# One fused decoder block on one core: a broadcast load moved behind a weight load, the work around the values' products reordered, two products swapped, upper values at other steps

## The chip, the core and the metric

The kernel runs on one core of a Trainium2 chip. A core has five engines with an instruction queue each: TensorE (PE, matmuls), VectorE (DVE), ScalarE (ACT), GpSimd (POOL) and SyncE (SP), which here only issues transfers. An engine works through its queue in order, and waits on semaphores for the others. The metric is the device time of one execution in microseconds; lower is better.

## The reference

One block of a decoder on 1024 tokens of 1024 features, in float32. The input is normalised (RMSNorm) and projected to queries, keys and values of 8 heads, to `u` and `vg` of a gated MLP, and to 8 forget logits. Forgetting attention, chunked spatial gating, and then a gated MLP with a causal convolution follow:

```python
xn = rmsnorm(h, norm_mix_g[layer])
proj = xn @ w_in[layer]                       # q, k, v, u, vg, forget logits
log_f = jax.nn.log_sigmoid(proj[..., G_END:] + b_forget[layer])
att = forgetting_attention(q, k, v, log_f)    # softmax(q k^T / 8 + c_i - c_k, causal) v, c = cumsum(log_f)
u, vg = split(jax.nn.gelu(proj[..., V_END:G_END]))
...
# gating: vg is normalised per group of 64 features, then per chunk of 128 tokens
w = w_s * jnp.tril(jnp.ones((CHUNK, CHUNK)))
mixed = jnp.einsum('gij,bnjgd->bnigd', w, vc) + b_s.T[None, None, :, :, None]
sg = u * mixed
h = h + jnp.concatenate([att, sg], axis=-1) @ w_out[layer]
h = h + conv_ffn(rmsnorm(h, norm_ffn_g[layer]), ...)   # (silu(g) * a) @ w_down, width-3 causal conv before
return rmsnorm(h, norm_final_g)
```

The change touches the part from the end of the `u`, `vg` and value projections to the first attention heads; the MLP behind it stays as it is.

## The kernel before

**Products.** Each float32 operand is split into a high part and a low part in the matmul's own type: ScalarE copies the high part (`act.copy`, line 157), VectorE subtracts it to get the low part (line 163). A product is then three matmuls: high by high, high by low, low by high. Many products are built as in Strassen's scheme: sums and differences of quarter matrices are multiplied, and the results added. The names T1 to T4, B11 to B22 stand for such quarters of the activations, and S1 to S4, A11 to A22 for those of a weight. `tmul` (line 267) multiplies one chunk of 128 rows, `product` (line 515) one quarter of the query and key weights, `vmul` (line 845) one of the values.

**Values, first half.** `wva` (two loads) and `wvk` hold weights for the values and the forget logits (264 columns, of which the last 8 are the logits). `vsum` adds two parts of them; `high` and `low` split them. T3-half and B22-half (matmuls of 264 columns, line 267) multiply them into the banks `S` and `S2`. Around them stand the gates: `gelu` on ScalarE, squares on ScalarE and group sums (`reduce`) on VectorE, a square root and a reciprocal of `gms`, and `norm`, which multiplies `vg` by it. `copies` stores the partial values and the logits (`vx`, `zf`). `rb` is 1/rms of every token, broadcast to all partitions: ScalarE stores it to `rbd` in HBM, SyncE loads it back (line 411). `emit` multiplies the keys and queries by it.

**Queries and keys.** `Weights(i)` loads a quarter of the query and key weights (two loads of 512 KB), `sums` and `last_sum` add quarters on GpSimd (lines 537 to 547), `split` splits them. `q1`, `q2` and four `qk_step` compute queries and keys of four pairs of heads, by products into the banks qa to qd. `forget` makes the log-sigmoid of the logits (table loads, Exp, Ln on ScalarE), `forget_sums` its running sums (matmuls at lines 601 and 602).

**Values, second half, and gating.** Weights `wvl` give the three products S2 x T2, A22 x T4 and S1 x T1 (line 845). Their results, with the partial values from `vx`, become values of the lower tokens (stored as `vd`, read back) and of the upper four heads (stored to `vu`). `evac_v` scales a tile of values into V: high part on ScalarE (line 733), low part on VectorE (line 737). `spatial` (line 792) multiplies eight groups of `vg` by the masked spatial weights `ws`, and gates `u` with the result: the first half on VectorE (`A<-pb`), the second half on ScalarE (into a temporary `pt`) and GpSimd (line 802). `turn_sg` transposes it (line 815), and the first head's logits follow (lines 967 and 968).

**Heads.** Each head has five steps with logits, softmax parts (`CUSTOM_DVE` at line 980, Exp at line 990), transposes (line 1015) whose results are split (lines 1016 and 1017) and products with V (line 1031). In steps 5 to 12 one tile of the upper four heads' values goes through `evac_v`.

**What sets the order.** While `act.on` and `dve.on` are true, each ScalarE or VectorE instruction is tied behind the one that the program wrote before it, so the order in the text is the order on the engine. With them false, the scheduler orders by its own costs, and `after(tc, later, earlier)` adds a single edge. `behind(inst, key)` ties to a gate stored under a key. SyncE issues loads and stores in the order of the text, as their buffers come free: `raw` has four buffers, `whl` four, `wy` two, `pt` three; a new tile of a name waits for the last reader of the buffer that it takes. Banks of `bank` and `sbank` are four each.

Of the kernel before, what the change touches and what calls it, by code (L numbers as in the profile page):

```python
# [14 lines left out]
P = 128  # L15
# [7 lines left out]
FCFG = ("b", 4, 4)  # L23

# [42 lines left out]
def block_kernel(ctx: ExitStack, tc: tile.TileContext, xT, xtok, wuv, wv0, wva, wvk, wvl, wqk, cpk, bfv,  # L67
# [341 lines left out]
    rb = sb("t01", [P, 1024])  # L409
    act.dma_start(out=rbd.rearrange("a p -> p a"), in_=rstd1)  # L410
    sp.dma_start(out=rb, in_=rbd.rearrange("a b -> (a b)").unsqueeze(0).to_broadcast((P, 1024)))
# [58 lines left out]
    w3 = [high(own_[0][:, k, :], 264) for k in range(2)]  # L470
    reduce(sq[0], 1, 0)
# [3 lines left out]
    for k in range(2):  # L475
        low(w3[k], own_[0][:, k, :])
    reduce(sq[1], 1, 2)
    w3 += [high(own_[0][:, k, :], 264) for k in (2, 3)]
    sq = [square(0, 0), square(0, 2)]
    dve.tensor_tensor(out=va[1][:, 0:1056], in0=va[0][:, 0:1056], in1=va[1][:, 0:1056], op=ALU.add)  # L480
    vsum(1)
    for k in (2, 3):
        low(w3[k], own_[0][:, k, :])
    reduce(sq[0], 0, 0)
    w4 = [high(own_[1][:, 0, :], 264)]
    reduce(sq[1], 0, 2)
    low(w4[0], own_[1][:, 0, :])
    act.activation(gms, gms, AF.Sqrt, bias=eps[:, 0:1], scale=1.0 / 64)
    dve.reciprocal(gms, gms)
# [3 lines left out]
    w4.append(high(own_[1][:, 1, :], 264))  # L493
    low(w4[1], own_[1][:, 1, :])
    for m in range(4):
        dve.tensor_tensor(out=ut[1][:, m, :], in0=B[m], in1=ut[1][:, m, :], op=ALU.subtract)
    for k in (2, 3):
        w4.append(high(own_[1][:, k, :], 264))
        behind_ = low(w4[k], own_[1][:, k, :])
    for m in range(4):  # L500
        gelu(ut[1][:, m, :], 4 + m)
    for hf in (1, 0):
        for t in (0, 2):
            norm(hf, t)
# [3 lines left out]
    copies(S, vx[1], 1)  # L508
# [10 lines left out]
    class Weights:  # L519


        def __init__(self, i):
            self.a, self.b = sb("raw", [P, 2, 512]), sb("raw", [P, 2, 512])
            sp.dma_start(out=self.a, in_=wqk[i, :, 2:4, :])
            sp.dma_start(out=self.b, in_=wqk[i, :, 0:2, :])
# [25 lines left out]
    W[0].split("A11", "A12")  # L551
    W[0].sums(behind_)
# [4 lines left out]
    act.on = dve.on = False  # L557
# [8 lines left out]

    qa = q1(0, "c")
    q2 = psq("a")
    product(q2, W[0].w["A12"], "B21", True)
# [13 lines left out]
    def forget_sums(c, r):  # L583
# [7 lines left out]
        act.activation(e, e, AF.Exp, scale=-1.0)  # L591
        x = act.activation(e, e, AF.Ln, bias=one[:, 0:1])
# [25 lines left out]
    fg = forget()  # L618
    tq, tk = sb("G", [P, 2, 1024]), sb("G", [P, 2, 1024])

    def emit(t, dst, i, parts, src=None):
        for o in parts:
            if dst is kd:
                dve.tensor_tensor(out=t[:, 1, o], in0=t[:, 1, o], in1=rb[:, o], op=ALU.mult)
            x = t[:, 1, o] if src is None else src
            act.copy(t[:, 0, o].bitcast(F32R), x)
            dve.tensor_tensor(out=t[:, 1, o], in0=x, in1=t[:, 0, o], op=ALU.subtract)
            for j in range(2):
                sp.dma_start(out=dst[2 * i + j].rearrange("s d t -> d s t")[:, :, o], in_=t[j * 64:(j + 1) * 64, :, o])
# [16 lines left out]
    def qk_step(i, qa, nxt):  # L646
# [5 lines left out]
        dve.tensor_tensor(out=u2, in0=qb, in1=x1, op=ALU.subtract)  # L652
        qc = psq("c")
        product(qc, w.w["S3"], "T3", True)
        dve.tensor_tensor(out=tk[:, 1, hi], in0=u2, in1=qc, op=ALU.add)
        w.split("S1")
        if i > 0:
            product(qa, w.w["A12"], "B21", False)
            emit(tq, qd, i, (lo,), qa)
        else:  # L660
# [6 lines left out]
        if i == 3:  # L667
            gates["keys"] = d
# [15 lines left out]
        if i == 3:  # L684
            gates["queries"] = d
# [6 lines left out]
    def gate_gain(hf):  # L692
# [3 lines left out]
        for t in (0, 2):  # L696
            v = vgt[hf][:, t:t + 2, :]
            behind(dve.tensor_tensor(out=v, in0=v, in1=gg[0].unsqueeze(1).to_broadcast((P, 2, 512)), op=ALU.mult), "queries")

    W[0].split("S2", "S3")  # L700
    fsum = forget_sums(*fg)
    next(fsum)
    for i in range(4):
# [6 lines left out]
    behind(dve.tensor_tensor(out=l21, in0=l21, in1=l22, op=ALU.add), "keys")  # L710
    behind(dve.tensor_tensor(out=l11, in0=l11, in1=l21, op=ALU.add), "keys")

    def pairs(t, gate=None):
        return [tsplit(t[:, 512 * j:512 * j + 512], gate, tag="whl") for j in range(2)]

    vw = {"S2": pairs(l11, "keys"), "A22": pairs(l22, "queries")}
    gate_gain(0)
# [3 lines left out]
    for i in range(2):  # L721
# [1067 lines left out]
```

## Time and profile before

| | |
|---|---|
| median of three executions | 1066.36 us (1063.12 to 1066.54) |
| profiled execution, its own time | 1066.44 us |
| its span in the profile | 1064.7 us |
| TensorE busy | 1043.8 us (98%) |
| VectorE busy | 892.9 us (84%) |
| ScalarE busy | 564.2 us (53%) |
| GpSimd busy | 223.5 us (21%) |
| mean granted TensorE clock | 0.996 |

The profile shows one execution. A row of a timeline gives the start in us from the span's start, the duration, the engine, the line, the operation with its output and inputs, and how many like it follow in a row; in brackets stands the idle time of the engine before it and the instruction that ended the wait. Names are those of the program's buffers, not of its variables: the banks of TensorE are `pb`, `ps`, `qa` to `qd`, `pl`; `G` holds among others the weights `wva` and the gates `vg`, `A` the gates `u`, `x` the value sums, `raw` loaded weights, `whl` and `wy` split ones. Lines 45 and 52 are the helper that ties instructions, so many operations have that line. A row of the table of stretches gives its bounds, then for each engine its busy time and, in brackets, its instructions, and at the end the granted clock, the busy share of the transfers and GB/s.

### The profile page before, as it was taken

What the parts mean: (1) busy time and instruction counts of PE and PEld (TensorE: products, weight loads), DVE (VectorE), ACT (ScalarE), POOL (GpSimd) and SP (SyncE); (2) the same over time, 40 slices, a digit from 0 to 9 for tenths busy, and PEclk for the clock granted to TensorE, in tenths of its full rate; (3) what the DMA queues carried; (4) which work ended last, traced back from release to release, by engine and by line L of the source; (5) the groups of instructions that cost most, each with busy time, mean ns of one, the idle gap of its engine ahead of it and who ended that gap; (6) DMA issues with size and microseconds to landing.
All of it is one profiled execution on the core that took longest, in us unless ns stands there. A gap on an engine that the chain in (4) does not pass through costs nothing.

```text
span 1064.7 us, 14262 instructions
## 1 busy us (share of the span) xinstructions
PE 1043.8 (98%) x4997; PEld 873.1 (82%) x4997; DVE 892.9 (84%) x1298; ACT 564.2 (53%) x1003; POOL 223.5 (21%) x169
## 2 busy tenths in 40 slices
PE   9999999989999999999999999999999999999997
PEld 6988888878888888888888888888888888888886
DVE  6897786878878869998999989989998775998774
ACT  6776532356866746654444444444444454444654
POOL 0000331230410740054333333323322000000000
PEclk9999999999999999999999999999999999999999
DMA  9624358768456345132344423322321899433342
GB/s 325 234 10 170 106 164 237 219 200 233 142 164 176 128 150 201 65 99 99 99 140 161 155 88 110 109 93 95 123 106 62 286 333 308 128 94 96 139 127 100
DMA packets 68491, 161.66 MB, mean 152 GB/s; under 512 B 9142, under 2 KB 10278, under 8 KB 68420
## 3 DMA queue, kind: packets, MB, share of 16 engines
q1 hardware_dynamic: 67108, 160.71, 47.5%
q8 instruction: 39, 0.64, 0.3%
q14 instruction: 32, 0.26, 0.1%
q10 hardware_dynamic: 1312, 0.04, 0.1%
HBM read 115.68 MB, written 45.05 MB: 151 GB/s over the span
## 4 chain that ended last, share of the span: by engine, by line
PE 83%; DVE 8%; ACT 4%; DMA 2%; issue 2%; SPq 0%; POOL 0%; ACTq 0%; DVEq 0%
PE k L1602 20%; PE qc L1342 11%; PE qa L1342 11%; PE qd L1342 11%; PE qb L1342 5%; PE pb L1031 2%; PE pb L1015 2%; PE ps L267 2%; PE pl L967 1%; PE pl L968 1%; PE pf L1055 1%; PE qc L515 1%; PE pf L1056 1%; PE pf L1057 1%; PE qd L515 1%
## 5 line engine op out<-in xcount | busy, mean ns | idle before, releaser
L1602 PE MATMUL k<-whb,wha 128*128 128x512 f32 (+1 forms) x936 | 209.9, 386 | 0.0
L1602 PEld LDWEIGHTS k<-whb,wha 128*128 128x128 f32 x936 | 174.1, 188 | 35.8 <-DVE wha L163 0.2
L1342 PE MATMUL qc<-xT,whb 128*128 128x512 f32 x540 | 129.9, 389 | 0.2 <-ACT whb L157 0.2
L1342 PE MATMUL qa<-xB,wha 128*128 128x512 f32 x528 | 127.4, 390 | 0.0
L1342 PEld LDWEIGHTS qc<-xT,whb 128*128 128x128 f32 x540 | 101.3, 188 | 21.6 <-ACT whb L157 0.5
L1342 PEld LDWEIGHTS qa<-xB,wha 128*128 128x128 f32 x528 | 98.8, 188 | 20.8 <-DVE wha L163 0.4
L157 ACT CAST wha<-sg 128x512 fp32r<-128x512 f32 x77 | 47.8, 622 | 96.6 <-PE k L1602 86.1
L157 ACT CAST whb<-sg 128x512 fp32r<-128x512 f32 x82 | 50.5, 618 | 87.6 <-PE qc L1342 67.3
L163 DVE TENSOR_TENSOR wha<-sg,wha 128x512 fp32r<-128x512 f32 x77 | 52.8, 688 | 38.8 <-ACT wha L157 38.7
L1342 PE MATMUL qd<-xB,whb 128*128 128x512 f32 x264 | 63.7, 389 | 0.0
L1342 PE MATMUL qd<-xT,whb 128*128 128x512 f32 x264 | 63.7, 389 | 0.0
L1016 ACT CAST pt<-pb 128x512 fp32r<-128x512 f32 x72 | 40.4, 585 | 41.1 <-PE pb L1015 34.6
L1342 PE MATMUL qb<-xT,whb 128*128 128x512 f32 x252 | 61.0, 389 | 0.0
L163 DVE TENSOR_TENSOR whb<-sg,whb 128x512 fp32r<-128x512 f32 x82 | 57.0, 697 | 4.4 <-ACT whb L157 4.3
L1226 POOL TENSOR_TENSOR sg<-raw 128x512 f32<-128x512 f32 x20 | 30.7, 1533 | 140.3 <-DVE whb L163 80.2
L1342 PEld LDWEIGHTS qd<-xT,whb 128*128 128x128 f32 x264 | 49.5, 188 | 10.5 <-DVE u L1449 0.3
L1342 PEld LDWEIGHTS qd<-xB,whb 128*128 128x128 f32 x264 | 49.5, 188 | 10.3
L1017 DVE TENSOR_TENSOR pt<-pb,pt 128x512 fp32r<-128x512 f32 x72 | 47.4, 687 | 11.0 <-ACT pt L1016 10.9
L1342 PEld LDWEIGHTS qb<-xT,whb 128*128 128x128 f32 x252 | 47.2, 188 | 10.1 <-DVE whb L163 0.3
L1031 PE MATMUL pb<-pt,V 128*128 128x512 f32 (+3 forms) x192 | 50.1, 365 | 0.4 <-DVE pt L1017 0.3
L1229 POOL TENSOR_TENSOR sg<-sg,raw 128x512 f32<-128x512 f32 x20 | 33.3, 1666 | 63.4 <-DVE whb L163 63.4
L1227 POOL TENSOR_TENSOR sg<-sg,raw 128x512 f32<-128x512 f32 x20 | 35.1, 1757 | 47.2 <-issue 44.6
(406 smaller groups left out, 2256.3 us busy)
## 6 DMA issues: line engine op xcount, KB each, us to landing
raw<-wup SPq DMA_DIRECT2D x44, 512.0 KB
sg<-hx SPq DMA_DIRECT2D x77, 256.0 KB
hx<-hs SPq DMA_DIRECT2D x44, 256.0 KB
hx<-ca SPq DMA_DIRECT2D x35, 256.0 KB
xT<-wdn SPq DMA_DIRECT2D x28, 256.0 KB
x<-kd SPq DMA_DIRECT2D x24, 256.0 KB
A<-xtok SPq DMA_DIRECT2D x8, 512.0 KB
raw<-wqk SPq DMA_DIRECT2D x8, 512.0 KB
```

The source lines that it names most:

```text
L157: act.copy(h, src)
L163: return eng.tensor_tensor(out=l, in0=src, in1=f32(h), op=ALU.subtract)
L267: pe.matmul(banks[m], xs(n, xi, k)[:, ms], w[:, wi, :], start=(first and k == 0 and c == 0 and (own or m % 2 == 0)), stop=(k == 3 and c == ...
L515: pe.matmul(ps, w[:, wi, ks], xs(n, xi, k), start=(first and c == 0), stop=(c == 11), skip_group_check=True)
L1016: casts.append(act.copy(pt[:, 0, :], ptr))
L1017: los.append(dve.tensor_tensor(out=pt[:, 1, :], in0=ptr, in1=f32(pt[:, 0, :]), op=ALU.subtract))
L1031: seq(pe.matmul(po[half][:, o:o + w], lhs, pt[:, s, c:c + w], start=(new and s == 0), stop=(s == 1 and (half, k) in ((1, 6), (0, 3))), ski ...
L1226: pool.tensor_tensor(out=s[0], in0=a21, in1=a22, op=ALU.add)
L1227: pool.tensor_tensor(out=s[1], in0=s[0], in1=a11, op=ALU.add)
L1229: pool.tensor_tensor(out=s[3], in0=s[1], in1=a12, op=ALU.add)
L1342: pe.matmul(ps, w[:, wi, ks], xb[:, xi, k, :], start=(first and n == 0), stop=(n == 11), skip_group_check=True)
L1602: pe.matmul((banks[bk + m] if ps is None else ps)[:, o], xh[:, xi, ms], wh[:, wi, o], start=((first and p_ == 0 or new) and n == 0), stop= ...
```

## The change

1. The load of `rb` is issued behind both loads of W[0] instead of ahead of the second `wva`.
2. From the `vsum(0)` on, VectorE's and ScalarE's order is rewritten: the lows of a weight come directly behind its highs, reductions between them; the subtractions of `ut[1]` stand ahead of the last three lows; the square root, reciprocal, norms and `copies` move behind the split of W[0]'s A11. W[0]'s sums on GpSimd lose their floor. The norms of `vgt[1]` come before the split of S2, those of `vgt[0]` behind `q2`. `forget` and the first `forget_sums` are made before `q1`, with the order still tied.
3. In the last step the gates become floors at single instructions; `l21` and `l11` are summed earlier, and the gains of `vgt[0]` come in two pieces. S2 and S1 are split ahead of the values' products, A22 during the first. `vx[1:3]` is one load.
4. The products S1 x T1 and A22 x T4 are swapped, and with them what is computed into `va_` and `vc_`.
5. The loads of `wos`, `wsp` and the stores of `ncd` are issued earlier; the low parts of four values move into `spatial`, between its gates.
6. The upper values go through `evac_v` at steps 4 to 8 and 13 to 15 instead of 5 to 12.

VectorE's queue between T3-half and B22-half, before (`gms` reductions, `wy` and `whl` lows of the weights in `G_821`, `A` the subtractions of `ut[1]`, `G_187` the norms):

```order
L52 TENSOR_REDUCE gms<-pt_928 128x16
L52 TENSOR_TENSOR wy_936<-G_821,wy_936 128x264
L52 RECIPROCAL gms<-gms 128x64
L52 TENSOR_TENSOR wy_994<-G_821,wy_994 128x264
L52 TENSOR_TENSOR A_189<-ps_194,A_189 128x512
L52 TENSOR_TENSOR A_189<-ps_195,A_189 128x512
L52 TENSOR_TENSOR A_189<-ps_196,A_189 128x512
L52 TENSOR_TENSOR A_189<-ps_197,A_189 128x512
L52 TENSOR_TENSOR whl_1001<-G_821,whl_1001 128x264
L52 TENSOR_TENSOR whl_1004<-G_821,whl_1004 128x264
L52 TENSOR_TENSOR G_187<-G_187,gms 128x1024 x2
```

The same stretch after the change (`G_819` is the weight, `raw_1059` is W[0]'s first load, so the last row but one is the low of A11):

```order
L55 TENSOR_TENSOR wy_985<-G_819,wy_985 128x264
L55 TENSOR_REDUCE gms<-pt_922 128x16
L55 TENSOR_REDUCE gms<-pt_924 128x16
L55 TENSOR_TENSOR A_189<-ps_194,A_189 128x512
L55 TENSOR_TENSOR A_189<-ps_195,A_189 128x512
L55 TENSOR_TENSOR A_189<-ps_196,A_189 128x512
L55 TENSOR_TENSOR A_189<-ps_197,A_189 128x512
L55 TENSOR_TENSOR wy_990<-G_819,wy_990 128x264
L55 TENSOR_TENSOR whl_996<-G_819,whl_996 128x264
L55 TENSOR_TENSOR whl_1002<-G_819,whl_1002 128x264
L55 TENSOR_TENSOR whl_1065<-raw_1059,whl_1065 128x512
L55 RECIPROCAL gms<-gms 128x64
```

The second low and the reciprocal have moved from ahead of the subtractions to behind them.

What follows there on VectorE, ahead of the additions into `zf` that read the banks of B22-half, before (four norms in two rows, then the lows of A11 and A12):

```order
L52 TENSOR_TENSOR G_187<-G_187,gms 128x1024 x2
L52 TENSOR_TENSOR G_186<-G_186,gms 128x1024 x2
L52 TENSOR_TENSOR whl_1081<-raw_1077,whl_1081 128x512
L52 TENSOR_TENSOR wy_1084<-raw_1077,wy_1084 128x512
L52 TENSOR_TENSOR zf<-ps_1015,zf 128x8
```

and after (the lows of A12 and of S2 around the two norms of `vgt[1]`):

```order
L55 TENSOR_TENSOR whl_1070<-raw_1059,whl_1070 128x512
L55 TENSOR_TENSOR G_187<-G_187,gms 128x1024 x2
L55 TENSOR_TENSOR wy_1089<-gg_1073,wy_1089 128x512
L55 TENSOR_TENSOR zf<-ps_1007,zf 128x8
L55 TENSOR_TENSOR zf<-ps_1008,zf 128x8
```

Two norms have left this stretch, and the low of S2, whose source `gg_1073` is a sum of GpSimd's, has come into it.

VectorE's queue at the end of the values' products and the start of `spatial`, before (`x` and `pt` take the products from the banks `ps`, `V` are lows of values, `A<-pb` the gates):

```order
L52 TENSOR_TENSOR x_195_1723<-ps_1870,x_195_1723 128x512
L52 SCALAR_TENSOR_TENSOR V_1923<-x_195_1723,rstd_109,V_1923 128x4x64 x2
L52 TENSOR_TENSOR x_195_1723<-x_195_1723,ps_1870 128x512
L52 TENSOR_TENSOR x_195_1723<-ps_1871,x_195_1723 128x512
L52 SCALAR_TENSOR_TENSOR V_1924<-x_195_1723,rstd_109,V_1924 128x4x64 x2
L52 TENSOR_TENSOR x_195_1723<-x_195_1723,ps_1871 128x512
L52 SCALAR_TENSOR_TENSOR A_188<-pb_1956,cp_75,A_188 128x4x64
L52 SCALAR_TENSOR_TENSOR A_188<-pb_1962,cp_75,A_188 128x4x64
```

and after:

```order
L55 SCALAR_TENSOR_TENSOR V_1731<-wy_1729,rstd_109,V_1731 128x4x64 x2
L55 SCALAR_TENSOR_TENSOR V_1732<-wy_1729,rstd_109,V_1732 128x4x64 x2
L55 TENSOR_TENSOR x_193_1717<-x_193_1717,ps_1861 128x512
L55 TENSOR_TENSOR x_193_1717<-x_193_1717,ps_1862 128x512
L55 SCALAR_TENSOR_TENSOR A_188<-pb_1949,cp,A_188 128x4x64
L55 SCALAR_TENSOR_TENSOR A_188<-pb_1956,cp,A_188 128x4x64
L55 SCALAR_TENSOR_TENSOR V_1940<-x_193_1717,rstd_109,V_1940 128x4x64
L55 SCALAR_TENSOR_TENSOR A_188<-pb_1964,cp,A_188 128x4x64
```

The lows of the lower values stand ahead of the last product's two sums now, and the four lows behind them are spread between the gates.

The diff, cut to what the prediction speaks of:

```diff
-    rb = sb("t01", [P, 1024])
     act.dma_start(out=rbd.rearrange("a p -> p a"), in_=rstd1)
-    sp.dma_start(out=rb, in_=rbd.rearrange("a b -> (a b)").unsqueeze(0).to_broadcast((P, 1024)))
...
+    w3 = [high(o0[k], 264) for k in range(2)]
+    for k in range(2):
+        low(w3[k], o0[k])
     for m in range(4):
         dve.tensor_tensor(out=vgt[0][:, m, :], in0=ut[1][:, m, :], in1=S[m], op=ALU.add)
         gelu(vgt[0][:, m, :], m)
...
+    vsum(1)
+    reduce(sq[1], 1, 2)
+    w4 = [high(o1[0], 264)]
+    low(w4[0], o1[0])
+    reduce(sq[2], 0, 0)
+    reduce(sq[3], 0, 2)
...
     for m in range(4):
         dve.tensor_tensor(out=ut[1][:, m, :], in0=B[m], in1=ut[1][:, m, :], op=ALU.subtract)
-    for k in (2, 3):
-        w4.append(high(own_[1][:, k, :], 264))
-        behind_ = low(w4[k], own_[1][:, k, :])
...
     W = [Weights(0)]
-    W[0].split("A11", "A12")
-    W[0].sums(behind_)
+    rb = sb("t01", [P, 1024])
+    after(tc, sp.dma_start(out=rb, in_=rbd.rearrange("a b -> (a b)").unsqueeze(0).to_broadcast((P, 1024))), W[0].d)
+    W[0].split("A11")
+    act.activation(gms, gms, AF.Sqrt, bias=eps[:, 0:1], scale=1.0 / 64)
+    dve.reciprocal(gms, gms)
+    W[0].split("A12")
+    W[0].sums()
+    copies(S, vx[1], 1)
+    norm(1, 0)
+    norm(1, 2)
+    W[0].split("S2")
     W[0].last_sum()
     copies(S2, vx[2])
...
-    W[0].split("S2", "S3")
-    fsum = forget_sums(*fg)
+    fsum = forget_sums(*forget())
     next(fsum)
+    W[0].split("S3")
+    qa = q1(0, "c")
+    q2 = psq("a")
+    product(q2, W[0].w["A12"], "B21", True)
+    norm(0, 0)
+    norm(0, 2)
+    next(fsum)
+    act.on = dve.on = False
...
+    after(tc, sp.dma_start(out=xy, in_=vx[1:3].rearrange("a p c -> p a c")), floors["ld"])
+    for i, o in ((0, ALU.subtract), (1, ALU.add)):
+        after(tc, dve.tensor_tensor(out=xy[:, i], in0=xy[:, i], in1=xl, op=o), newest[0])
+    vw["S1"] = pairs(l21)
...
+    vw["A22"] = [tsplit(l22[:, hw[0]], tag="whl")]
     for j, o in enumerate(hw):
         dve.tensor_tensor(out=va_[:, o], in0=Q[j], in1=va_[:, o], op=ALU.add)
         dve.tensor_tensor(out=vb_[:, o], in0=Q[j], in1=vb_[:, o], op=ALU.subtract)
-    vw["S1"] = pairs(l21)
+    vw["A22"].append(tsplit(l22[:, hw[1]], tag="whl"))
+    vmul(R, vw["S1"], "T1")
     Q = [sbank() for _ in range(2)]
     vmul(Q, vw["A22"], "T4")
-    R = [sbank() for _ in range(2)]
-    vmul(R, vw["S1"], "T1")
...
+            if g < 2:
+                vlow.append(evac_v(6 + g, 0, vb_[:, (2 + g) * 256:(2 + g) * 256 + 256]))
+            if 1 <= g < 5:
+                vlow[g - 1]()
...
-        if 5 <= n < 13:
-            low = evac_v(n - 5, 1, vh[:, (n - 5) // 4, (n - 5) % 4, :])
+        if n in UPPER:
+            tt = UPPER.index(n)
+            low = evac_v(tt, 1, vh[:, tt // 4, tt % 4, :])
             after(tc, low(), los[-1])
             after(tc, vhigh[0], exs[-1])
```

`UPPER` is `(4, 5, 6, 7, 8, 13, 14, 15)`.

More of the change, by code (lines that the diff above doesn't have):

```diff
@@ L709, in block_kernel, with pairs @@
         sp.dma_start(out=t, in_=wvl[i])
[L710 to L717, printed above, removed]
+    after(tc, dve.tensor_tensor(out=l21, in0=l21, in1=l22, op=ALU.add), floors["u", 3])
+    after(tc, dve.tensor_tensor(out=l11, in0=l11, in1=l21, op=ALU.add), floors["k", 3])
+    after(tc, gate_gain(0, (0,)), floors["k", 3])
+    after(tc, gate_gain(0, (2,)), floors["q", 3])
+    def pairs(t):
+        return [tsplit(t[:, 512 * j:512 * j + 512], tag="whl") for j in range(2)]
+    vw = {"S2": pairs(l11)}
     xy = sb("x1", [P, 2, 1024])
```

107 lines of the change are left out of this document (44 added, 63 removed).

## The prediction

> **What bounds the kernel now.** I read the page's busy shares first, then TensorE's timeline for its gaps, then, for each gap, the timelines of the engines that end it.
>
> ```profile
> PE 1043.8 (98%) x4997; PEld 873.1 (82%) x4997; DVE 892.9 (84%) x1298; ACT 564.2 (53%) x1003; POOL 223.5 (21%) x169
> ```
>
> TensorE is busy for 1043.8 of 1064.7 us. The change neither adds nor removes a matmul, so it can move the time only through the 20.9 us of idle and through matmuls that run at a lower clock. The gaps that it touches lie in three places (start us, duration, then in brackets the idle before and what ended it):
>
> ```profile
> 94.60 3.19 PE L267 MATMUL pb<-whl,x 128*128 128x264 f32 x25
> 97.97 3.07 PE L267 MATMUL pb<-whl,x 128*128 128x264 f32 x23 [0.19 <-DVE whl L52]
> 102.52 5.12 PE L267 MATMUL ps<-wy,t 128*128 128x264 f32 x24 [1.47 <-DVE A L52]
> 107.43 3.32 PE L267 MATMUL ps<-whl,t 128*128 128x264 f32 x24
> 110.59 2.88 PE L515 MATMUL qc<-V,whl 128*128 128x512 f32 x12
> 124.87 0.30 PE L602 MATMUL pb<-gg 128*128 128x64 f32 x1 [0.49 <-DVE gg L45]
> 126.36 3.00 PE L515 MATMUL qc<-V,whl 128*128 128x512 f32 x12 [0.96 <-DVE G L45]
> ...
> 189.98 5.90 PE L845 MATMUL ps<-whl,H 128*128 128x256 f32 x47 [0.51 <-DVE whl L45]
> 203.13 5.89 PE L845 MATMUL ps<-whl,H 128*128 128x256 f32 x47 [1.34 <-DVE whl L52]
> 208.86 3.62 PE L792 MATMUL pb<-G,pt 128*128 128x256 f32 x16
> 215.74 3.72 PE L792 MATMUL pb<-G,pt 128*128 128x256 f32 x16 [3.27 <-ACT pt L52]
> 219.30 1.91 PE L815 MATMUL ps<-ident,A 128*128 128x128 f32 x16
> 223.40 0.50 PE L967 MATMUL pl<-x 128*128 128x512 f32 x1 [0.44 <-DVE G L52]
> ...
> 282.92 0.66 PE L1015 MATMUL pb<-ident,t 128*128 128x128 f32 x4 [0.95 <-DVE pt L1017]
> 284.78 0.50 PE L967 MATMUL pl<-x 128*128 128x512 f32 x1 [0.73 <-DVE mn L980]
> ```
>
> The twenty-four matmuls at 102.52 took 5.12 us, those at 107.43 only 3.32. The table of stretches tells why (before DMA share and GB/s stands the granted clock):
>
> ```profile
> 104.60:107.90 3.30, 3.30 (x18) 3.30 (x17) 3.30 (x4) 3.30 (x12) 0.00 (x0) 0.50 0.03 12
> 285.50:288.80 3.30, 3.30 (x15) 2.85 (x14) 3.30 (x6) 2.19 (x6) 0.95 (x1) 0.50 0.49 160
> 212.50:215.70 3.20, 0.00 (x0) 0.00 (x0) 3.20 (x6) 0.48 (x2) 1.41 (x2) 1.00 0.03 13
> ```
>
> Twice the clock is at 0.50 for 3.3 us, which costs half of that, 1.7 us: after the 1.47 us gap at 102.5 and after the pair of 0.95 and 0.73 us at 283 to 285. It stays at 1.00 through and after the 3.27 us gap. The Trainium skill (TensorE: Matmul & The Clock Gate, "HAM oscillation") gives as the abstract rule no idle gaps over about 3.4 us; this trace differs, since 1.47 us sufficed. By that rule the gap of 2.5 us forecast below would keep its clock and the sum would stand; by the trace it may lose it, 1.7 us more, and that is a rival.
>
> **First place: the broadcast and the values' order.** VectorE, and what holds it:
>
> ```profile
> 82.93 0.96 DVE L52 TENSOR_TENSOR G<-G 128x768 f32<-128x768 f32 x1 [1.57 <-DMA G<-wva]
> 89.32 0.43 DVE L52 TENSOR_TENSOR G<-gg,G 128x256 f32<-128x256 f32 x1 [5.43 <-DMA gg<-wvk]
> ...
> 93.19 0.77 DVE L52 TENSOR_TENSOR whl<-G,whl 128x264 fp32r<-128x264 f32 x2
> ...
> 98.18 2.34 DVE L52 TENSOR_REDUCE gms<-pt 128x16 f32<-128x1024 f32 x2
> 101.69 2.47 DVE L52 TENSOR_TENSOR A<-ps,A 128x512 f32<-128x512 f32 x4
> ...
> 104.77 4.62 DVE L52 TENSOR_TENSOR G<-G,gms 128x1024 f32<-128x1024 f32 x4
> ...
> 114.84 1.77 DVE L45 TENSOR_TENSOR whl<-raw,whl 128x512 fp32r<-128x512 f32 x1
> 118.22 0.69 DVE L45 TENSOR_TENSOR whl<-raw,whl 128x512 fp32r<-128x512 f32 x1 [0.31 <-ACT whl L45]
> ```
> ```profile
> SPq L411 <- DMA rbd<-rstd: 9.0, 1, 9.0
> ```
> ```profile
> 82.90:89.30 6.40, 6.40 (x30) 5.31 (x29) 0.96 (x1) 0.73 (x2) 0.00 (x0) 1.00 0.99 380
> ```
>
> In SyncE's queue the broadcast waits 9.0 us for the small store `rbd`; the second `wva` (912 KB) and `wvk` (256 KB) are queued behind it, and VectorE waits 5.43 us for `wvk`. Moved behind W[0]'s loads, the broadcast holds neither. The first `wva` was there at 82.93. At the 380 GB/s of the last row the two loads' 1.20 MB take 3.15 us, so `wvk` is there at 86.1 and VectorE goes on 3.2 us earlier. The bounds are the broadcast's 512 KB at that rate, 1.4 us, and the whole wait, 5.4; I take 3.2, the sum by bytes. The broadcast itself is first read in `emit`, behind four more products of 2.88 us from 110.59, so after 120; its own delay is free.
>
> From there to the subtractions of `ut[1]` (the `A<-ps,A` rows) VectorE had 11.9 us of work, 89.75 to 101.69. The new order keeps the reductions ahead of them but takes out the reciprocal and puts one low before the second sums; I leave it at 11.9: subtractions from 98.4 to 100.9. TensorE is through the half product before it at 100.85 (97.97 + 3.07, less the 0.19 us gap), 6.25 us after 94.60. The banks are free in time, the lows of `w4` (0.385 each, by the row at 93.19) follow by 102.1, and the first of them is due a quarter into the next half product, at 102.4. So B22-half starts at 100.85 and, at full clock, ends at 107.1, where q1 now starts at 110.59: 0.19 + 1.47 + 1.7 us and the slack between them, **3.5 us gained**.
>
> Then comes a new wait. W[0]'s sums on GpSimd lose their floor, and start behind the low of A11, near 103.5 (102.1, its cast on ScalarE and 0.69 us). On VectorE stand the low of A12, two norms, the low of S2 and only then the four `zf` additions that free the bank for q2:
>
> ```profile
> 113.07 1.30 POOL L541 TENSOR_TENSOR raw<-raw 128x512 f32<-128x512 f32 x1
> 114.32 1.75 POOL L547 TENSOR_TENSOR raw<-gg,raw 128x512 f32<-128x512 f32 x1
> ```
>
> The low at 114.84 took 1.77 us while GpSimd ran, the same one at 118.22 0.69 without it: both engines, reading two operands in SBUF, take turns. The Trainium skill (SBUF — State Buffer, "SBUF: two separate sides") calls the shared port pair an exclusive lock for the whole instruction; the trace agrees (1.77 against 0.69 us). Without that lock its sum would be the lower bound of the next sentence. Alone, 0.69 + 2 x 1.155 + 0.69 us end at about 107.7 and the `zf` additions at 108.3, before TensorE is through q1 at 109.8: no gap. In turns with GpSimd's four sums (1.3 us each) they need 8.9 us and end near 112.4. I take the second, since the row at 114.84 went that way: **2.5 us lost** ahead of q2 (0 to 2.6). ScalarE's table loads then start earlier than now, and the lows of S1 come at about 120.3, when qd is due; the gaps of 0.49 and 0.96 us close: **1.45 gained**. First place: 3.5 - 2.5 + 1.45 = 2.45 us; with the bounds, from 0 (broadcast worth 1.4, B22-half's gap and slow clock kept) to 4.95.
>
> **Second place: the values' products and the gating.** S1 and S2 are split before the products, so Q and R run on without the 0.51 us gap; A22 is split during them and the third product's 1.34 us gap goes. Three products of 5.75 us from 189.2 end at 206.45 instead of 208.86: 2.4 us. The swap itself costs nothing; Q's banks are free by 196, 4.7 us before the third product. The large gap is VectorE's:
>
> ```profile
> 211.54 2.65 DVE L52 SCALAR_TENSOR_TENSOR V<-x,rstd,V 128x256 fp32r<-128x256 f32 x2 [0.58 <-ACT V L52]
> 214.71 1.65 DVE L52 SCALAR_TENSOR_TENSOR A<-pb,cp,A 128x256 f32<-128x256 f32 x4
> ...
> 215.22 1.65 ACT L52 ACTIVATE pt<-pb,cp 128x256 f32<-128x256 f32 x4 [3.31 <-DVE A L52]
> ...
> 220.83 1.56 ACT L52 CAST G<-ps 128x512 fp32r<-128x512 f32 x3
> ```
>
> The first four gates (L52 `A<-pb`) wait behind four lows of V and four sums that need the last product. Now only two sums need it; four lows stand ahead of these sums, in time that waits for the product, and four between the gates, so the banks come free as spatial runs: 206.45 + 3.62 + 3.6 = 213.7, transposes 3.66 us (219.30 to 222.96) to 217.4. What is late next: the second temporary takes the slot of the spatial weights, so ScalarE's last four gates start only after the last spatial matmul, and their 1.65 us, four casts (0.52 each) and the last low (0.69) reach 218.2 to 218.4, where logits start. From 223.40 that is **5.0 us gained** (6.0 without that wait; 2.4 if the lows and GpSimd's splits of `wos`, taking turns, keep the 3.27 us gap).
>
> **Third place: the upper values.**
>
> ```profile
> 278.09 2.17 ACT L157 CAST whl<-raw 128x512 fp32r<-128x512 f32 x4
> 280.16 0.51 ACT L733 ACTIVATE V<-A,rstd 128x256 fp32r<-128x256 f32 x1
> ...
> 280.70 1.56 DVE L737 SCALAR_TENSOR_TENSOR V<-A,rstd,V 128x256 fp32r<-128x256 f32 x1 [1.69 <-ACT V L733]
> ...
> 294.07 0.69 DVE L1058 TENSOR_TENSOR raw<-pf,raw 128x512 f32<-128x512 f32 x1 [0.90 <-PE pf L1057]
> ```
>
> VectorE stood 1.69 us because the high half of V was queued behind four casts on ScalarE. Steps 9 to 12 have no such pair now: the gaps of 0.95 and 0.73 us and the slow 3.3 us behind them go, 1.68 + 1.7 = **3.4 us**. One pair moves to step 4 and three to steps 13 to 15, where VectorE has gaps (0.90 at 294.07); covered, they cost nothing, uncovered about 0.5 to 1.6 us each, so 0 to 3.4 stay.
>
> **The sum** is 2.45 + 5.0 + 3.4 = 10.9 us; the profiled execution took 1066.44, so 1055.5. It lies 0.08 us from the median, 1066.36. A change under 0.3%, 3.2 us, could not be told from none.
>
> **The rivals.**
> - *Thinner gain.* The gap before q2 halves the clock (1.7 us more), `wvk` comes only 1.4 us earlier, or spatial's or the upper values' wait comes back: each leaves 6 to 9.3 us. For it: the 1.47 us gap did so at 102.52; against it: the 3.27 us one did not. About 1059.
> - *No new gap.* VectorE gets past GpSimd and q2 starts at once: 2.5 us more, 1053. Against it stands the row of 1.77 us.
> - *Nothing carries over.* `wvk` is held as long as now by the slow first `wva`, and the slack in spatial is refilled by VectorE's turns with GpSimd: 0 + 2.4 us and a third place whose gap only moves: 1064.
> - *Slower: a transfer late for the products.* `xy` becomes one load of 1 MB behind the last step's q-low stores in SyncE's queue. It takes 2.8 us at 380 GB/s and is due when the first product ends at 195; each later microsecond holds the third product, the gates and the logits, one for one. It decides once it lands 14 us late, near 209: 1070 or so. The queue's longest hold above, 9.0 us, speaks for it; against it, that these stores leave by 184 (SyncE's row below), 8 us before it must be under way.
>
> ```profile
> 182.62 1.24 SPq L629 DMA_DIRECT2D qd<-G  x2
> ```
>
> **How the numbers follow.** Forecast 0.42, thinner gain 0.24, no new gap 0.12, nothing carried over 0.10, slower 0.12. Faster is the first three, 0.78. The bounds add to 0 + 2.4 + 0 = 2.4 and 4.95 + 6.0 + 3.4 = 14.35 us gained, that is 1064.0 and 1052.1; with a microsecond for the scatter of executions at the lower end, 1051 to 1064.2 leaves out the slower case and little else.
>
> **What would show it.** Right: `wvk` ending VectorE's wait near 86; q1 near 107 at clock 1.00 and q2 about 2.5 us behind it, released by `zf`; spatial without a gap; logits' start 7 to 8 us earlier than 223.4 in all; no gap near 283, and clock 1.00 after it. It is wrong if the 0.50 stretches turn up elsewhere, if TensorE waits at qd for S1's lows, or if steps 13 to 15 bring gaps behind L737's successor.

## The result and the profile after

| | before | after |
|---|---|---|
| median of 15 executions each | 1066.36 us (1063.12 to 1068.72) | 1061.72 us (1059.75 to 1063.98) |
| ratio | | 0.996, 95% interval 0.9949 to 0.997 |
| span of the profiled execution | 1064.7 us | 1061.2 us |
| TensorE busy | 1043.8 us | 1045.6 us |
| mean granted clock | 0.996 | 0.993 |

The kernel became faster, by 4.6 us; the forecast was 10.9. TensorE's busy time rose though its matmuls are the same ones: more of them ran at half clock. The profiled execution has the lowest mean clock of the fifteen, 0.993 (two have it); their median is 0.995. The waits of TensorE after the change (us in total, times, longest):

```profile
PE qa L512 <- DVE zf L55: 2.8, 1, 2.8
PE pb L825 <- POOL A L808: 2.1, 3, 0.7
PE ps L126 <- DVE pad L137: 1.3, 1, 1.3
PE pb L1024 <- DVE pt L1026: 0.9, 1, 0.9
PE pb L1024 <- DVE raw L1067: 0.7, 1, 0.7
PE pl L976 <- DVE mn L989: 0.7, 1, 0.7
```

Of the waits of before, those of the spatial matmuls for `pt` (3.3 us), of B22-half for `A` (1.5) and of the values' products for `whl` (1.3 and 0.5) are gone; the two largest here are new. TensorE's timeline at the places of the forecast:

```profile
94.05 5.97 PE L270 MATMUL pb<-whl,x 128*128 128x264 f32 x48
99.87 3.07 PE L270 MATMUL ps<-wy,t 128*128 128x264 f32 x24
105.68 2.88 PE L512 MATMUL qc<-V,whl 128*128 128x512 f32 x12
111.40 4.38 PE L512 MATMUL qa<-x,whl 128*128 128x512 f32 x12 [2.84 <-DVE zf L55]
124.14 2.99 PE L512 MATMUL qc<-V,whl 128*128 128x512 f32 x12
...
204.35 7.07 PE L798 MATMUL pb<-G,pt 128*128 128x256 f32 x32
...
214.58 0.66 PE L825 MATMUL pb<-ident,A 128*128 128x128 f32 x4 [0.72 <-POOL A L808]
...
217.32 1.12 PE L825 MATMUL pb<-ident,A 128*128 128x128 f32 x4 [0.71 <-POOL A L808]
218.09 0.78 PE L976 MATMUL pl<-x 128*128 128x512 f32 x1
...
236.41 1.85 PE L1024 MATMUL pb<-ident,t 128*128 128x128 f32 x12 [0.72 <-DVE raw L1067]
...
282.87 0.50 PE L976 MATMUL pl<-x 128*128 128x512 f32 x1 [0.66 <-DVE mn L989]
```

Where TensorE's idle time went in the profiled pair is read by setting the start of the same matmul in both timelines side by side; the difference is what has been gained up to there:

| matmul | before | after | gained so far |
|---|---|---|---|
| T3-half, ahead of the change's effects (start-up differs) | 94.60 | 94.05 | 0.55 |
| q1 | 110.59 | 105.68 | 4.9 |
| q2 | 113.31 | 111.40 | 1.9 |
| second product into qc (A22) | 126.36 | 124.14 | 2.2 |
| spatial | 208.86 | 204.35 | 4.5 |
| first logits | 223.40 | 218.09 | 5.3 |
| nine matmuls into the output projection | 229.03 | 227.00 | 2.0 |
| transposes of the second gap near 283 | 282.92 | 281.14 | 1.8 |
| end | 1064.7 | 1061.2 | 3.5 |

Between the first logits and 227 nothing waits for long, and yet 3.3 us are lost. The table of stretches (before DMA share and GB/s the granted clock) shows why:

```profile
111.00:114.30 3.30, 2.90 (x7) 2.32 (x8) 2.06 (x11) 2.78 (x6) 1.08 (x1) 0.50 0.02 5
216.80:226.90 10.10, 9.51 (x25) 7.45 (x26) 5.88 (x10) 4.73 (x9) 2.93 (x3) 0.50 0.58 159
282.00:285.00 3.00, 2.35 (x13) 1.85 (x13) 3.00 (x6) 2.74 (x5) 3.00 (x3) 1.00 0.34 111
```

The clock is at 0.50 for 3.4 us behind q2's gap and for 10.2 us behind the three gaps among the transposes. The stretch near 285 is gone.

What ends the three gaps is GpSimd. Its queue and ScalarE's:

```profile
207.55 1.36 POOL L162 CAST whl<-raw 128x512 fp32r<-128x512 f32 x2 [9.42 <-DMA raw<-wos]
208.88 2.90 POOL L166 TENSOR_TENSOR whl<-raw,whl 128x512 fp32r<-128x512 f32 x2
211.75 5.52 POOL L808 TENSOR_TENSOR A<-pt,A 128x256 f32<-128x256 f32 x8
```
```profile
205.94 0.48 ACT L55 ACTIVATE pt<-pb,cp 128x256 f32<-128x256 f32 x1 [3.35 <-DVE A L55]
```

ScalarE has the first gate's input ready at 206.4, but GpSimd's eight gates (L808) stand behind its two splits of `wos`, whose load lands only at 207.5. They run in one piece from 211.75 to 217.2, 0.69 us each, and TensorE takes them two by two. This order is one line of the program, `after(tc, x, splits[0])`, and the kernel before has it too. There it cost nothing: the splits ended at 213.9, and the gates behind them still waited 1.86 us for ScalarE:

```profile
211.24 2.67 POOL L163 TENSOR_TENSOR whl<-raw,whl 128x512 fp32r<-128x512 f32 x2
215.77 4.86 POOL L802 TENSOR_TENSOR A<-pt,A 128x256 f32<-128x256 f32 x7 [1.86 <-ACT pt L52]
```

### The profile page after: what moved, and what is told of

Same layout as the page of the kernel before. It is cut to its first block, busy times and chain, and to the rows that moved or that the text cites. A ratio compares the mean times of both kernels' runs of the same rounds, so it can differ in the third digit from the quotient of the medians.

```text
span 1061.2 us, 14270 instructions
## 1 busy us (share of the span) xinstructions
PE 1045.6 (99%) x4997; PEld 873.4 (82%) x4997; DVE 892.4 (84%) x1298; ACT 564.7 (53%) x1002; POOL 224.0 (21%) x169
## 4 chain that ended last, share of the span: by engine, by line
PE 82%; DVE 5%; ACT 3%; issue 1%; DMA 0%; POOL 0%; ACTq 0%; DVEq 0%; SPq 0%
PE k L1612 20%; PE qc L1352 11%; PE qd L1352 11%; PE qa L1352 10%; PE qb L1352 5%; PE pb L1040 3%; PE pb L1024 2%; PE qd L512 2%; PE qc L512 2%; PE qa L512 2%; PE ps L855 2%; PE pl L976 1%; PE pl L977 1%; PE pf L1064 1%; PE pf L1065 1%; PE pf L1066 1%
```

## The experiments

Every ratio is to the kernel before, run on the same chip alongside. There the kernel before had medians of 1064.85 to 1066.69 us, so the ratios compare better than the times.

| run | median us | ratio | 95% interval |
|---|---|---|---|
| changed kernel (15 executions) | 1061.72 | 0.996 | 0.9949 to 0.997 |
| e1 gates first | 1055.89 | 0.9898 | 0.9872 to 0.9923 |
| e2 norms later | 1057.44 | 0.9914 | 0.9888 to 0.994 |
| e7 two sums out | 1057.33 | 0.991 | 0.9883 to 0.9936 |
| e8 keep busy | 1057.08 | 0.9911 | 0.9879 to 0.9942 |
| e3 upper values back | 1061.81 | 0.9973 | 0.9956 to 0.999 |
| e4 gates and norms | 1054.51 | 0.9899 | 0.9868 to 0.9929 |
| e5 broadcast alone, in the kernel before | 1063.09 | 0.9978 | 0.9961 to 0.9995 |
| e6 upper values alone, in the kernel before | 1063.19 | 0.9984 | 0.9965 to 1.0004 |
| e9 three edits | 1053.08 | 0.9885 | 0.9868 to 0.9903 |
| e10 three edits, upper values back | 1056.29 | 0.9917 | 0.9901 to 0.9933 |
| e11 swap back | 1060.43 | 0.995 | 0.9931 to 0.997 |
| e12 three edits, norms in the steps | 1052.75 | 0.988 | 0.9864 to 0.9895 |

**GpSimd's gates ahead of its splits.**

```diff
-    for k in range(2):
-        whs.append(sg_split(wrs[k], "pool"))
...
-                after(tc, x, splits[0])
+                gated[:] = [x]
...
+    for k in range(2):                       # behind the transposes of the first half, in the text
+        t = sb("whl", [P, 2, 512], F32R)
+        after(tc, pool.tensor_copy(t[:, 0], wrs[k]), gated[0])
+        pool.tensor_tensor(out=t[:, 1], in0=wrs[k], in1=f32(t[:, 0]), op=ALU.subtract)
...
```

> The changed kernel, with GpSimd's eight gates ahead of its two splits of wos instead of behind them. Theory: the gates were late only because they stood behind the splits, and the three gaps of 0.72 us that this opens between the transposes also put the clock at 0.50 for the 10.2 us behind them. Then the gaps go, the logits start near 216, the clock stays at 1.00, and the time falls by 2.1 + 5.1 us, to about 1054.5. Rival: the slow stretch has nothing to do with these gaps; then only 2.1 us go, 1059.6, and the clock is at 0.50 after the transposes as before. Second rival: the splits, now later, hold the first matmuls of the output projection; then a gap of 1 to 2 us appears near 219.

```profile
208.72 2.11 POOL L808 TENSOR_TENSOR A<-pt,A 128x256 f32<-128x256 f32 x3 [0.58 <-ACT pt L55]
211.00 0.74 POOL L808 TENSOR_TENSOR A<-pt,A 128x256 f32<-128x256 f32 x1 [0.17 <-ACT pt L55]
211.68 1.17 POOL L923 CAST whl<-raw 128x512 fp32r<-128x512 f32 x2
...
211.07 1.91 PE L825 MATMUL pb<-ident,A 128*128 128x128 f32 x16
213.38 0.50 PE L979 MATMUL pl<-x 128*128 128x512 f32 x1 [0.39 <-DVE G L55]
```

The transposes run in one piece, the clock stays at 1.00, and the median falls by 5.8 us (5.1 us of clock and 2.1 us of gaps were in the profile). The splits, 4 us later, hold nobody. This shows the cause of the second place's loss; it doesn't tell gap and clock apart. Not all of the difference is the edit's: the logits start 4.7 us earlier than in the changed kernel, but 1.9 of them are there when spatial starts (202.42 against 204.35), since q2's gap was 2.23 us this time and left the clock at 1.00.

**The same waits with TensorE kept busy.** Three matmuls of 512 columns into the bank that the transposes overwrite:

```diff
+    def keep_busy(ps, n=3):
+        for _ in range(n):
+            seq(pe.matmul(ps, sgT[0][:, 0, 0:P], sgT[0][:, 0, 0:512], start=True, stop=True))
...
     for c in range(4):
-        pts.append(turn_sg(1, c, bank()))
+        pt_ = bank()
+        if c:
+            keep_busy(pt_)
+        pts.append(turn_sg(1, c, pt_))
```

> The changed kernel, with three matmuls of 512 columns put ahead of each of the last three groups of upper transposes; they write a bank that the transposes overwrite. GpSimd's gates stay late, so the transposes start when they did, but TensorE is busy in the gaps. Theory that idle time halves the clock: no stretch at 0.50 behind the transposes, logits near 218.1 at full speed, 5.1 us less, about 1057. Rival (the clock falls for what TensorE executes there, or by chance): 0.50 stays, and the time is 1061.7 or a little more.

```profile
212.39 0.94 PE L830 MATMUL pb<-G 128*128 128x512 f32 x3
...
216.55 0.48 PE L981 MATMUL pl<-x 128*128 128x512 f32 x1
```
```profile
216.60:226.00 9.40, 8.67 (x41) 6.97 (x40) 7.50 (x14) 5.31 (x10) 1.96 (x2) 1.00 0.79 251
```

The gates stand behind the splits as before (5.57 us in one piece), and the last transposes start at 216.14, as the last gate ends; so the added work cost next to nothing, yet the clock is at 1.00 and the median 4.6 us lower. In all four profiles in which these gaps stay empty (the changed kernel, e2, e3 and e7) a stretch at half clock follows them. So idle time among the transposes is what halves the clock. Not all of the 4.6 us comes from there: VectorE's order in the first head came out otherwise here, and the gap of 0.72 us at 236.41 is not there, about 1 us; and in the profile q2's gap of 2.33 us kept its clock.

**The two norms behind the additions.**

```diff
-    norm(1, 0)
-    norm(1, 2)
     W[0].split("S2")
...
         dve.tensor_tensor(out=zf[:, 4 + m, 0:8], in0=S2[m][:, 256:264], in1=zf[:, 4 + m, 0:8], op=ALU.add)
+    norm(1, 0)
+    norm(1, 2)
```

> The changed kernel, with the two norms of vgt[1] behind the zf additions instead of ahead of them. Theory: the gap of 2.84 us ahead of q2 is the time of these two norms (4.5 us, stretched by GpSimd's sums), and the clock's 3.4 us at 0.50 follow from the gap. Then q2 starts right behind q1, no slow stretch at 111, and the time falls by 2.8 + 1.7 us to about 1057.2. Rival: the low of S2, which waits for GpSimd and is still ahead of zf, holds the additions anyway; then a gap of 1 to 2 us stays and with it, perhaps, the clock; 1059 to 1061.

The median is the one expected, 1057.44, but only part of the reason given holds. `zf` is added at 107.24, and q2 follows q1 without a gap:

```profile
107.24 0.37 DVE L55 TENSOR_TENSOR zf<-ps,zf 128x8 f32<-128x8 f32 x4
107.53 3.15 DVE L55 TENSOR_TENSOR G<-G,gms 128x1024 f32<-128x1024 f32 x2
...
118.34 3.29 PE L512 MATMUL qd<-H,whl 128*128 128x512 f32 x12 [0.80 <-ACT whl L160]
```

A wait of 0.80 us turned up at qd, where the forecast had S1's lows arriving just in time. So spatial starts 2.3 us earlier than in the changed kernel (202.06 against 204.35), not 4.5. The gaps among the transposes grew to 3.2 us, and the rest of the difference in the profiles is mainly the slow stretch behind them, which lasted 3.41 us here and 10.24 there. That the number agreed is in part luck.

**Two of GpSimd's sums left out.** In `sums` of W[0] the sum for S1 and in `last_sum` the one for S4 are left out; these products then take unsummed weights.

```diff
-    W[0].sums()
+    W[0].two_sums()        # a11 + a21, and that + a22; no third sum
...
-    W[0].last_sum()
```

> The changed kernel, with the last two of GpSimd's four sums of W[0] left out (the sums for S1 and S4 of the first query and key weights; these products take unsummed weights instead). Nothing else moves. Theory of the taking of turns: with GpSimd quiet from 105.7 on, the two norms take 1.16 us each instead of 2.25, zf is added by about 109, and the gap ahead of q2 is 0.4 us or less instead of 2.84; without the slow stretch too the time is about 1057.5. Rival: the norms are slow for another reason (their operands, their shape), and the gap stays at 2.8 us, 1061.5.

VectorE's norms after the change, and here:

```profile
106.15 4.51 DVE L55 TENSOR_TENSOR G<-G,gms 128x1024 f32<-128x1024 f32 x2
```
```profile
105.53 2.35 DVE L55 TENSOR_TENSOR G<-G,gms 128x1024 f32<-128x1024 f32 x2
108.40 0.37 DVE L55 TENSOR_TENSOR zf<-ps,zf 128x8 f32<-128x8 f32 x4
```

With GpSimd quiet the two norms take 2.35 us instead of 4.51, the gap ahead of q2 is gone, and spatial starts 4.1 us earlier (200.26 against 204.35). The turns with GpSimd are the cause of that gap, as forecast. Both this edit and the one before remove it; either is enough.

**The upper values back at steps 5 to 12.**

```diff
-UPPER = (4, 5, 6, 7, 8, 13, 14, 15)
+UPPER = (5, 6, 7, 8, 9, 10, 11, 12)
```

> The changed kernel with part 6 undone: the upper values at steps 5 to 12 again. Theory: what the third place gave in the changed kernel is the gap of 0.95 us near 283 and the slow 3.4 us behind it (1.7 us); both come back, and the time rises by 2.6 us to 1064.3. Rival: with the heads starting at another time the high half of V no longer meets the four casts; then nothing comes back, 1061.7. By the forecast's own term, 3.4 us, it would be 1065.1.

The median came out at 1061.81, the ratio 0.0013 above the changed kernel's, with overlapping intervals: not decided here. The profile does show the gap of 0.9 us and a slow stretch of 3.4 us behind it again. The same edit in the version with three edits decides it (below).

**Both edits together.**

> The changed kernel with both edits of the two runs before: GpSimd's gates ahead of its splits of wos, and the two norms behind the zf additions. Theory: the two losses are independent, so the gains add up (5.8 and 4.3 us, each alone): 1061.7 - 10.1 = 1051.6, with the clock at 1.00 from the start to the last product. Rival: once one gap is gone the other is covered in part by what waits behind it, and only 7 to 8 us are left: 1054.

The rival was right: 1054.51, a ratio of 0.9899 where the gates alone gave 0.9898. q2's gap is gone, 0.78 us wait at qd for a cast of ScalarE's, and in the profile of the gates alone q2's gap (2.23 us) had left the clock at 1.00.

**The broadcast alone, in the kernel before.** The load moved as in part 1, nothing else.

```diff
-    sp.dma_start(out=rb, in_=rbd.rearrange("a b -> (a b)").unsqueeze(0).to_broadcast((P, 1024)))
...
     W = [Weights(0)]
+    rb = sb("t01", [P, 1024])
+    after(tc, sp.dma_start(out=rb, in_=rbd.rearrange("a b -> (a b)").unsqueeze(0).to_broadcast((P, 1024))), W[0].d)
```

> The kernel before with part 1 alone: the broadcast behind W[0]'s loads, no order changed. Theory: the first weights for the values come 3.2 to 3.7 us earlier, VectorE's subtractions are done before TensorE needs their banks, and the gap of 1.47 us at 102.5 and the slow stretch behind it go: 3.3 us, 1063.0; the gaps of 0.49 and 0.96 us near 125 stay. Rival: without the new order VectorE has its norms and lows in the way, and the gap moves to q1 or q2: 1065.5 to 1066.4.

```profile
84.66 0.42 DVE L52 TENSOR_TENSOR G<-gg,G 128x256 f32<-128x256 f32 x1 [2.26 <-DMA gg<-wvk]
97.03 2.47 DVE L52 TENSOR_TENSOR A<-ps,A 128x512 f32<-128x512 f32 x4
...
99.65 3.07 PE L267 MATMUL ps<-wy,t 128*128 128x264 f32 x24
...
105.47 2.88 PE L513 MATMUL qc<-V,whl 128*128 128x512 f32 x12
...
121.68 3.00 PE L513 MATMUL qc<-V,whl 128*128 128x512 f32 x12 [0.96 <-DVE G L45]
```

VectorE's wait ends at 84.66 instead of 89.32, B22-half starts without a gap, q1 at 105.47, and the second product into qc at 121.68: 2.5 us earlier than in the changed kernel. The median, 1063.09, is the number expected, but the gain is not: it lies 1.8 us below the kernel before that ran alongside (1064.85), where 3.3 were expected. In this stretch the load alone does better than the load with the new order: the order closes the gaps of 0.7 and 0.96 us, and opens q2's.

**The upper values alone, in the kernel before.** `if 5 <= n < 13` becomes `if n in (4, 5, 6, 7, 8, 13, 14, 15)`.

> The kernel before with part 6 alone: the upper values at steps 4 to 8 and 13 to 15. Theory, from the changed kernel's trace: the gap of 0.95 us at 283 and the slow stretch behind it go, the gap of 0.73 us at 285 (a softmax minimum) stays: 2.6 us, 1063.8. By the forecast's term both gaps go: 1063.0. Rival: the pairs at steps 13 to 15 open gaps of their own: 1065 to 1066.4.

1063.19 and a ratio of 0.9984, whose interval holds 1: as a time not decided. In the profile the gap of 0.95 us is gone, that of the softmax minimum stays at 0.6.

**Three edits.** Gates first; the norms of `vgt[1]` behind the split of S3; and the first head's minimum over 256 columns tied behind two sums of the output projection:

```diff
     W[0].split("S3")
+    norm(1, 0)
+    norm(1, 2)
     qa = q1(0, "c")
...
-                dve.tensor_tensor(out=hs, in0=ps, in1=hs, op=ALU.add)
+                added.append(dve.tensor_tensor(out=hs, in0=ps, in1=hs, op=ALU.add))
...
+        if h == 0 and j == 1:
+            after(tc, m, added[1])
```

> The changed kernel with three edits: GpSimd's gates ahead of its splits of wos; the two norms of vgt[1] behind the forget logits' Exp and the split of S3, so that ScalarE's casts for S1 come earlier; and the first head's minimum over 256 columns tied behind the first two sums of the output projection. Theory: with both waits behind q1 gone and nothing late at qd, the gap of 0.78 us there goes too, and of the 0.99 us among the first head's transposes at least 0.7: 1.5 us below the version with the first edit and the norms behind zf (0.9899 of the kernel before), so a ratio of 0.988 to 0.989, 1052 to 1053. Rival: the gap at qd only moves to the first step's later products, and the ratio is 0.990.

```profile
118.48 2.57 PE L512 MATMUL qd<-H,whl 128*128 128x512 f32 x10 [1.79 <-DVE whl L166]
...
212.43 0.50 PE L979 MATMUL pl<-x 128*128 128x512 f32 x1 [0.39 <-DVE G L55]
```

The ratio, 0.9885, is the expected one, but not for the reason given: the gap at qd grew to 1.79 us, since now all four norms (4.62 us) stand ahead of S1's lows on VectorE. The gap at 236 is gone.

**The same with the upper values back.**

> The version of the run before, with the upper values at steps 5 to 12 again. Theory: part 6 is worth the gap of 0.95 us that comes back in step 10, and, in the executions in which that gap halves the clock, 1.7 us more: 1.0 to 2.6 us slower than the run before. By the forecast's term it would be 3.4 us. Rival: part 6 is worth nothing, since the run of the changed kernel without it had the same median; then the two are within 0.5 us.

3.2 us slower, the two sets of executions apart (1055.21 to 1058.55 against 1052.74 to 1053.61). The profile shows the gap and the clock behind it:

```profile
275.18 0.66 PE L1029 MATMUL pb<-ident,t 128*128 128x128 f32 x4 [0.93 <-DVE pt L1031]
...
277.03 0.58 PE L979 MATMUL pl<-x 128*128 128x512 f32 x1 [0.74 <-DVE mn L992]
```
```profile
120.40:123.60 3.20, 3.20 (x9) 2.42 (x9) 2.75 (x7) 0.62 (x1) 0.00 (x0) 0.50 0.47 134
277.40:280.70 3.30, 3.30 (x12) 2.74 (x11) 3.30 (x6) 2.55 (x6) 1.30 (x2) 0.50 0.46 160
```

The slow stretch of the second row costs 1.7 us and the gap of 0.93 us ahead of it makes that 2.6. The first row is a slow stretch behind a gap of 1.99 us at qd; in the profile of the three edits the gap there, 1.79 us, left the clock at 1.00. The profiled execution is also the slowest of its six (1058.55), so how much of the 3.2 us comes from such differences stays open.

**The swap back.** `vmul(Q, vw["A22"], "T4")` ahead of `vmul(R, vw["S1"], "T1")`, VectorE's order kept.

> The changed kernel with part 4 undone on TensorE: A22 x T4 ahead of S1 x T1; VectorE's order stays, apart from some softmax pieces of the first head that the scheduler orders anew. The forecast costed the swap at nothing, since Q's banks are free long before. Theory now: the swap hides the split of A22, whose lows end at 193.8 and 196.8 in the changed kernel, while the second product starts at 192.8; without the swap TensorE waits 1.0 us there, or more for the second half, and spatial's first gates wait for the last product as VectorE takes R's sums first: 1 to 2 us slower, 1063. Rival: no difference, 1061.7.

```profile
191.17 6.02 PE L855 MATMUL ps<-whl,V 128*128 128x256 f32 x47 [0.29 <-DVE whl L55]
...
209.79 5.49 PE L798 MATMUL pb<-G,pt 128*128 128x256 f32 x12 [3.82 <-ACT pt L55]
```

The theory's gap for A22's split is 0.29 us, not 1.0, and the time isn't worse (0.995 against 0.996, within the intervals). But the profile shows what the swap does: without it the spatial matmuls wait 3.82 us for their banks again, since VectorE's first gates stand behind sums that need the last product. With it that wait goes, and GpSimd's gates are the next in line. So what the swap saves at spatial, the changed kernel loses again at the late gates, as far as one profile of each can show it.

**The norms in the steps.** From the three edits, the norms go behind the sums of qd in steps 0 and 1:

```diff
-    norm(1, 0)
-    norm(1, 2)
...
-    norm(0, 0)
-    norm(0, 2)
...
         floors["d", i] = d
+        if i < 2:
+            for t_ in (0, 2):
+                after(tc, norm(1 - i, t_), d)
```

> The version with the three edits, but with the four norms taken out of the stretch ahead of qd: two behind step 0's qd, two behind step 1's. Theory: the gap of 1.79 us at qd was the 4.62 us of norms ahead of S1's lows on VectorE, and the steps have room for 2.3 us each, since VectorE waits there; the gap goes and nothing comes for it: a ratio of 0.987, 1.8 us below the three edits (0.9885). Rival: VectorE is late for the first step's later products instead, and the gap moves there: a ratio of 0.988 to 0.990.

```profile
129.06 0.27 PE L612 MATMUL pb<-ident,gg 128*72 128x128 f32 x1 [0.91 <-DVE gg L607]
```

The gap at qd is gone, and half of it comes back as a wait of 0.91 us of the transpose of the running sums, for which VectorE is late. That is the rival. A ratio of 0.988: with 0.9885 the two can't be told apart. Both beat the kernel before and the changed one.

## Why the forecast was wrong, point by point

Direction and most mechanisms were right; the gain was 4.6 us of 10.9. The step that failed is the second place's term, 5.0 us: it followed ScalarE's part of the gates to its end and left out GpSimd's, which the two splits of `wos` hold back. The profiled pair gave -0.2 us there, less than the lower bound of 2.4.

- **The broadcast.** Right. VectorE's wait for `wvk` ended at 85.62 (forecast 86.1), B22-half started without a gap at 99.87, and up to q1 4.9 - 0.55 = 4.35 us were gained (forecast 3.5). The run with the load alone shows that this part does it, without the new order. That q2 then waits was forecast at 2.5 us and measured at 2.84, for the cause given (the run with two sums out). What was put into a rival instead of the sum is the clock: 3.4 us at 0.50 behind this gap, 1.7 us. The place gave 1.7 us (2.2 less 0.55 of start-up) instead of 2.45.
- **The values' products and the gating, forecast 5.0 us.** The products ran on as expected (spatial at 204.35, in one piece), and what it named as late next, ScalarE's last four gates behind the last spatial matmul, was late: 211.51. But behind them it took GpSimd's share as done when ScalarE's was. It counted the splits of `wos` only as a contender of VectorE's, not as what GpSimd's own gates are queued behind. The gates ended at 217.2, the transposes waited 2.1 us, and these gaps took 5.1 us of clock. Up to the first logits the place gave 3.1 us (5.3 less 2.2), and 2.0 - 2.2 = -0.2 us once the clock was back. The profiled execution shows the dear case: with one piece of half clock instead of three, as in the profiles of e2, e3 and e7, the place would have given about 3.2 us (an estimate: -0.2 plus two pieces of 1.7). The run with the gates first shows that the order on GpSimd is the cause, and the run with TensorE kept busy that the clock follows the idle time. The rows of before held the warning: the splits ended only 1.86 us ahead of the gates there. ScalarE's first gate came 9.3 us earlier after the change (205.94 against 215.22), the splits only 2.6 (207.55 against 210.10).
- **The upper values, forecast 3.4 us.** The size was off. Of the two gaps only the 0.95 us went; that behind the softmax minimum stayed at 0.66. The slow stretch went (1.65). Against that, VectorE's order in the first head, which no step of the forecast looked at, opened 0.72 and 0.27 us at 236. Together 1.5 us in the profiled pair. Taking part 6 out of the version with three edits cost 3.2 us, of which its own place explains at most 2.6.
- **The clock as a term.** The sum booked two slow stretches of one profiled execution as certain gains. Across 25 executions of the kernel before (those beside e3 to e6) the mean clock ran from 0.993 to 0.999, and across the 15 of the changed kernel from 0.993 to 0.998. One stretch of 3.41 us is 0.0016 of it: such stretches come and go between executions of one kernel, and each is worth 1.7 us.
- **The rivals.** The thinner gain is the nearest, with one of its named triggers (the gap before q2 halves the clock) and one that it did not name; but it left 6 to 9.3 us, and 4.6 were measured. The median does lie in the stated range, 1051 to 1064.2, but not by the route of its bounds, which gave the second place 2.4 us at least. That `xy` lands late did not come about: VectorE's subtraction of `xl` ran at 190.8, ahead of its need. The swap, costed at nothing, removes a wait of 3.8 us (swap back); the forecast had put that to VectorE's order alone.

## What to carry to other kernels

When a chain of work passes through several engines, walk each engine's own queue up to the last link: here ScalarE's part was followed and GpSimd's, one step behind it, was taken as free, though two splits that waited for a load stood ahead in its queue. A short wait of TensorE should be priced twice, with and without a stretch of half clock behind it, and a slow stretch of a single profile is not a sure gain. If a wait can't be removed at once, matmuls whose result is overwritten can keep the clock up: with nine of them in the gaps the clock stayed at 1.00 here, and the median fell by 4.6 us, about 1 us of it from another cause.

## What the runs showed of the hardware

- **The clock falls in pieces of 3.41 us on a grid of its own.** By the traces' clock records, slow stretches lasted 3.41 us (before, after, and the runs e2, e3, e7, e10), 6.83 us (e11) and 10.24 us (after). Within one profile their starts lie whole multiples of 3.413 us apart: 53.0 in the kernel before, 31.0 in the changed kernel (105.81 us), 31.0 and 19.0 in e3, 46.0 in e10. The Trainium skill (TensorE: Matmul & The Clock Gate, "What's actually happening") describes a free-running window of 3413 ns; the runs agree. The Trainium skill's rule of no idle gaps over about 3.4 us (TensorE: Matmul & The Clock Gate, "HAM oscillation") is too mild for this kernel: gaps of 2.84 us, of 1.47 us, and three of 0.72 us within 3.5 us each had a stretch at half clock behind them.
- **The length of a gap alone does not decide.** q2's gap halved the clock at 2.84 us and in e3 at 2.09 us (the first row below), and not at 2.23 and 2.33 us (the profiles of e1 and e8); 3.27 us between spatial matmuls did not in the kernel before, 3.82 us at the same place did in e11. A gap's place on the grid would explain that, but no run here sets it. Nor is it known why the three small gaps cost three pieces in the changed kernel and one in e3 and e7, with the same gaps, and in e2, with 3.2 us of gaps (the second row):

```profile
110.29 4.62 PE L512 MATMUL qa<-x,whl 128*128 128x512 f32 x12 [2.09 <-DVE zf L55]
```
```profile
216.40:219.60 3.20, 3.20 (x10) 2.61 (x9) 0.78 (x1) 0.59 (x1) 2.04 (x2) 0.50 1.02 239
```

- **VectorE and GpSimd take turns.** Two norms with both operands in SBUF took 2.35 us alone and 4.51 us beside GpSimd's sums, and GpSimd's sums 1.75 and 2.24 us instead of 1.3:

```profile
105.62 1.76 POOL L538 TENSOR_TENSOR raw<-raw 128x512 f32<-128x512 f32 x1
107.34 2.24 POOL L544 TENSOR_TENSOR raw<-gg,raw 128x512 f32<-128x512 f32 x1
```
